# FFN of a hybrid encoder block in two parts of its width, with 36 pairs of its row blocks by seven products of sums

## The chip, the cores and the metric

The kernel runs on one core of one Trainium2 chip. The metric is the device time of one execution in microseconds (us). PE is TensorE, whose weight loads have rows of their own (PEld); DVE is VectorE, ACT is ScalarE, POOL is GpSimd, and SP issues most transfers (its queue is SPq).

## What is computed

One encoder block over x (1 x 256 x 2048, fp32): a pre-RMSNorm, one wide projection, a Hyena branch (long convolution with filters from a small network) and a gated SGU branch, merged by sigmoid gates and a projection, then the feed-forward part that most of the change is about:

```python
h = _rmsnorm(x, norm_ffn_g[l])
gate, up = jnp.split(jnp.einsum('bsd,df->bsf', h, w_ffn_in[l]), 2, axis=-1)
x = x + jnp.einsum('bsf,fd->bsd', jax.nn.silu(gate) * up, w_ffn_out[l])
...
return _rmsnorm(x, norm_final_g)
```

D_MODEL is 2048 and D_FF is 5632, so `w_ffn_in` is 2048 x 11264 and `w_ffn_out` is 5632 x 2048. The 256 tokens are two blocks of 128 (tt = 0, 1).

## The kernel before

**Every product is three products.** An fp32 operand is written as two fp32r parts, hi (a cast, ACT) and lo (the operand less hi, DVE), and a product is hi x hi + hi x lo + lo x hi, accumulated in one PSUM bank of 128 x 512. `Net.tokens` (L127 to L134) issues these three matmuls for each token block: the stationary operand is a 128 x 128 block of the activations, the moving one a 128 x 512 block of the weights.

**Weights are a stream.** `Net.halves` lists every 128 x 1024 piece of weights in the order of use. `Net.feed` (L70 to L87) loads a piece by SP into a buffer `raw` and splits it by `split_to` (L65 to L68: the cast on ACT is L67, the subtraction on DVE L68) into `whi` and `wlo`. `Net.take(i)` (L89) first feeds five pieces beyond i. From the merge on there are six `raw` and six `whi`/`wlo` buffers (four in one pool and two in another, taken in turn), so that the split of piece k waits until PE has read piece k - 6, and the load of piece k until piece k - 6 has been split. Engines work through their instructions in order.

**Stages.** (1) `phase_a` (L452): the SGU half of the projection while x arrives, with its first row block of weights in two pieces of 512 columns, and then all other tiles of the projection, with the filters (`filt`, L509) and convolutions woven in by `hook`, one step at each tile. (2) The branch merge and the output projection (up to L367); each column block of the result is transposed on PE (`turn`, L155 to L162) through two of four `aux` banks, scaled and split into X2. (3) FFN in: 22 chunks, each with 256 columns of gate and 256 of up and 16 row blocks (`line_of`, L136). The chunks use two pairs of banks, `mm` and `mg`, in turn (`banks`, L291), so that a finished pair is read (silu on ACT, L391, the product with up on DVE, L392) while PE fills the other. Two chunks together are transposed two ticks later (a tick is the end of a weight piece in the loop) and split into H. (4) FFN out: four column blocks of 512, each over all 44 row blocks of H. In the last one the last four pieces are kept, so that token block 0 ends early. (5) The last RMSNorm: the sum of squares (L434), a reciprocal square root on DVE, four scalings and stores.

Of the kernel before, what the change touches and what calls it, by code (L numbers as in the profile page):

```python
# [38 lines left out]
class Net:  # L39
    def __init__(self, nc, tc, a):  # L40
        self.nc, self.tc, self.a = nc, tc, a
        self.halves = []
        self.parts = {}
        self.split_at = 0
        self.ws2 = None
        self.todo = []

# [21 lines left out]

    def feed(self, upto):  # L70
        nc = self.nc
        while self.split_at < min(upto, len(self.halves)):
            i = self.split_at
            src, w, kept = self.halves[i]
            pool, n = (self.ws, RAW_BUFS) if self.ws2 is None or i % 3 else (self.ws2, 2)
            raw = pool.tile([P, 1024], F32, name="raw", bufs=n)[:, 0:w]
            nc.sync.dma_start(out=raw, in_=src)
            if kept is None:
                pool, n = (self.ws, HL_BUFS) if self.ws2 is None or i % 3 else (self.ws2, 2)
                hi = pool.tile([P, 1024], F32R, name="whi", bufs=n)[:, 0:w]  # L80
                lo = pool.tile([P, 1024], F32R, name="wlo", bufs=n)[:, 0:w]
                self.split_to(hi, lo, raw)
                self.parts[i] = (hi, lo)
            else:
                hi, lo, view = kept()
                self.split_to(hi, lo, view(raw))
            self.split_at += 1  # L87

# [59 lines left out]
    def tick(self):  # L148

        for t in self.todo:  # L150
            t[0] -= 1
        while self.todo and self.todo[0][0] <= 0:
            self.todo.pop(0)[1]()
# [64 lines left out]

RAW_BUFS = 4
# [5 lines left out]
def build(nc, tc, a):  # L225
# [28 lines left out]
    fi_first = [net.line(a["wfi"][c], 8) for c in range(HF)]  # L254
    fo_first = [net.line(a["wfo"][n], HF) for n in range(4)]

    with ExitStack() as top:
        const = top.enter_context(tc.tile_pool(name="const", bufs=1))
        net.ws = top.enter_context(tc.tile_pool(name="ws", bufs=1))
        ev = top.enter_context(tc.tile_pool(name="ev", bufs=1))  # L260
        dram = top.enter_context(tc.tile_pool(name="dram", bufs=1, space=bass.MemoryType.DRAM))
        gate_d = dram.tile([8, 2, P, 512], F32, name="gate_d")
        y_d = dram.tile([2, P, D], F32, name="y_d")

# [12 lines left out]
        left = ExitStack()  # L277
        ys_pool = left.enter_context(tc.tile_pool(name="ys_pool", bufs=1))
# [57 lines left out]
        for n in range(4):  # L336
# [4 lines left out]
            if n == 0:  # L341

                net.line_of(ps, wo_first[0], 8, M, net.tick)
                left.close()
                x2s = ExitStack()
                x2pool = x2s.enter_context(tc.tile_pool(name="x2pool", bufs=1))
                X2 = x2pool.tile([P, KD, 512], F32R, name="X2")
            else:
                net.line_of(ps, wo_first[n], 8, M, net.tick)
            for tt in range(2):  # L350
# [18 lines left out]
        def rms(which, tts):  # L369

            n = len(tts)
            ms = ev.tile([P, n], F32, name="ms", bufs=2)
            nc.vector.tensor_reduce(out=ms, in_=ss[:, which, tts[0]:tts[0] + n, :], op=ALU.add, axis=AX.X)
            nc.vector.tensor_scalar(out=ms, in0=ms, scalar1=1.0 / D, scalar2=EPS, op0=ALU.mult, op1=ALU.add)
            return net.rsqrt_cols(ev, ms, n)
# [3 lines left out]
        H, two = None, []  # L379
        for c in range(HF):  # L380
            ps = banks()
            net.line_of(ps, fi_first[c], 8, X2, net.tick)
            if c == 0:
                inner.close()
                hpool = sd.enter_context(tc.tile_pool(name="hpool", bufs=1, side="right"))
                H = hpool.tile([P, NF, 512], F32R, name="H")
                nc.vector.tensor_copy(out=r2, in_=rms(0, (0, 1)))
            hs = []
            for tt in range(2):
                h = ev.tile([P, L], F32, name="t", bufs=T_BUFS)  # L390
                nc.scalar.activation(out=h, in_=ps[tt][:, 0:L], func=AF.Silu, scale=r2[:, tt:tt + 1])  # L391
                nc.vector.scalar_tensor_tensor(out=h, in0=ps[tt][:, L:2 * L], scalar=r2[:, tt:tt + 1], in1=h,  # L392
                                               op0=ALU.mult, op1=ALU.mult)
                hs.append(h)

            def to_h(pt, c=c):
                net.split_to(H[:, 2 * c:2 * c + 2, 0:L], H[:, 2 * c:2 * c + 2, L:2 * L], pt)
            two.append((hs, to_h))
            if c % 2:
                net.later(2, lambda two=two: net.turn([t[0] for t in two], [t[1] for t in two]))  # L400
                two = []

        for n in range(4):
            ps = banks()
            cut = HF if n < 3 else HF - TAILQ
            for q in range(cut):
                hi, lo = net.take(fo_first[n] + q)
                for e in range(2):
                    k = 2 * q + e
                    net.tokens(ps, hi, lo, 512 * e, H, k, k == 0, k == NF - 1)  # L410
                net.tick()
            if n == 0:
                x2s.close()
                gfp = sd.enter_context(tc.tile_pool(name="gfp", bufs=1))
                yacc = gfp.tile([P, 2, D], F32, name="yacc")
                for tt in range(2):
                    nc.sync.dma_start(out=yacc[:, tt, :], in_=y_d[tt])
                gB = gfp.tile([P, D], F32, name="gfB")
                nc.sync.dma_start(out=gB, in_=a["gfin"].partition_broadcast(P))
            sl = slice(512 * n, 512 * (n + 1))  # L420
            if n == 3:

                parts = [net.take(fo_first[n] + q) for q in range(cut, HF)]
            for tt in range(2):
                if n == 3:
                    for q in range(cut, HF):
                        hi, lo = parts[q - cut]
                        for e in range(2):
                            k = 2 * q + e
                            net.tokens(ps, hi, lo, 512 * e, H, k, False, k == NF - 1, (tt,))  # L430
                y = yacc[:, tt, sl]
                nc.vector.tensor_tensor(out=y, in0=ps[tt], in1=y, op=ALU.add)
                sq = ev.tile([P, 512], F32, name="sq", bufs=2)
                nc.scalar.activation(out=sq, in_=y, func=AF.Square, accum_out=ss[:, 1, tt, n:n + 1])  # L434
                if n < 3:
                    nc.vector.tensor_tensor(out=y, in0=y, in1=gB[:, sl], op=ALU.mult)
                else:

                    r = rms(1, (tt,))
                    for m in (0, 3, 1, 2):  # L440
                        y = yacc[:, tt, 512 * m:512 * (m + 1)]
                        if m == 3:
                            nc.vector.scalar_tensor_tensor(out=y, in0=y, scalar=r[:, 0:1], in1=gB[:, sl],
# [531 lines left out]
```

## Time and profile before

| | |
|---|---|
| median of 3 runs | 1389.6 us (1389.49 to 1389.66) |
| the profiled execution's own time | 1391.37 us |
| its span, first to last instruction | 1389.6 us |
| PE busy | 1376.4 us (99%), 6570 matmul records |
| weight loads (PEld) busy | 1151.7 us (83%) |
| DVE busy | 867.6 us (62%) |
| ACT busy | 658.1 us (47%) |
| moved by DMA | 276 MB, 199 GB/s on average |

A busy share is a mean over all stages. A matmul's record is longer than the distance to the next one (they overlap in the array), so the cost of a matmul is read from that distance. "Idle before" tells how long an engine had nothing to do ahead of an instruction, and the arrow names what it waited for.

### The profile page before, as it was taken

What the parts mean: (1) busy time and instruction counts of PE and PEld (TensorE: products, weight loads), DVE (VectorE), ACT (ScalarE), POOL (GpSimd) and SP (SyncE); (2) the same over time, 40 slices, a digit from 0 to 9 for tenths busy, and PEclk for the clock granted to TensorE, in tenths of its full rate; (3) what the DMA queues carried; (4) which work ended last, traced back from release to release, by engine and by line L of the source; (5) the groups of instructions that cost most, each with busy time, mean ns of one, the idle gap of its engine ahead of it and who ended that gap; (6) DMA issues with size and microseconds to landing.
All of it is one profiled execution on the core that took longest, in us unless ns stands there. A gap on an engine that the chain in (4) does not pass through costs nothing.

```text
span 1389.6 us, 17294 instructions
## 1 busy us (share of the span) xinstructions
PE 1376.4 (99%) x6570; PEld 1151.7 (83%) x6570; DVE 867.6 (62%) x1191; ACT 658.1 (47%) x819; POOL 0.7 (0%) x6
## 2 busy tenths in 40 slices
PE   9999999999999999999999999999999999999997
PEld 7888888888888888888888888888888888888885
DVE  7887798797888666556555554545455544545453
ACT  7665555555455444445444444444444443434342
POOL 0000000000000000000000000000000000000000
PEclk9999999999999999999999999999999999999999
DMA  8775656556555796677666665656565667666651
GB/s 293 243 240 179 189 173 200 153 184 219 166 164 170 253 317 200 205 231 213 195 184 190 187 194 187 194 184 196 186 192 183 195 219 251 197 188 194 194 182 60
DMA packets 82162, 276.00 MB, mean 199 GB/s; under 512 B 10144, under 2 KB 10912, under 8 KB 81696
## 3 DMA queue, kind: packets, MB, share of 16 engines
q1 hardware_dynamic: 79632, 270.64, 61.3%
q10 hardware_dynamic: 2448, 4.27, 0.8%
q8 instruction: 51, 0.84, 0.2%
q14 instruction: 31, 0.25, 0.0%
HBM read 266.49 MB, written 8.39 MB: 198 GB/s over the span
## 4 chain that ended last, share of the span: by engine, by line
PE 97%; DMA 1%; DVE 1%; ACT 0%; SPq 0%; issue 0%; ACTq 0%
PE mg L132 15%; PE mg L134 15%; PE mg L133 15%; PE mm L133 11%; PE mm L134 11%; PE mm L132 11%; PE mm L98 9%; PE mm L100 4%; PE aux L578 2%; PE aux L162 1%; PE aux L527 1%; PE aux L133 1%; PE aux L134 1%; PE aux L132 0%; DMA raw<-in_wsv 0%; PE aux L613 0%
## 5 line engine op out<-in xcount | busy, mean ns | idle before, releaser
L68 DVE TENSOR_TENSOR wlo<-raw,whi 128x1024 fp32r<-128x1024 f32 (+1 forms) x473 | 577.3, 1222 | 464.9 <-ACT whi L67 459.6
L67 ACT CAST whi<-raw 128x1024 fp32r<-128x1024 f32 (+1 forms) x473 | 496.5, 1051 | 619.9 <-PE mg L134 264.2
L132 PE MATMUL mg<-whi,X 128*128 128x512 f32 x608 | 237.9, 391 | 0.0
L134 PE MATMUL mg<-whi,X 128*128 128x512 f32 x608 | 236.9, 390 | 0.0
L133 PE MATMUL mg<-wlo,X 128*128 128x512 f32 x608 | 236.8, 389 | 0.0
L98 PE MATMUL mm<-X,whi 128*128 128x512 f32 x512 | 161.9, 397 | 0.0
L134 PE MATMUL mm<-whi,X 128*128 128x512 f32 x384 | 150.0, 391 | 0.0
L133 PE MATMUL mm<-wlo,X 128*128 128x512 f32 x384 | 149.9, 390 | 0.0
L132 PE MATMUL mm<-whi,X 128*128 128x512 f32 x384 | 149.7, 392 | 0.0
L134 PEld LDWEIGHTS mg<-whi,X 128*128 128x128 f32 x608 | 114.1, 188 | 24.0
L132 PEld LDWEIGHTS mg<-whi,X 128*128 128x128 f32 x608 | 114.1, 188 | 23.1 <-issue 0.4
L133 PEld LDWEIGHTS mg<-wlo,X 128*128 128x128 f32 x608 | 114.2, 188 | 22.8
L100 PEld LDWEIGHTS mm<-X,wlo 128*128 128x128 f32 x512 | 96.2, 188 | 22.6
L100 PE MATMUL mm<-X,wlo 128*128 128x256 f32 x512 | 100.8, 278 | 0.0
L134 PEld LDWEIGHTS mm<-whi,X 128*128 128x128 f32 x384 | 72.4, 188 | 15.1
L133 PEld LDWEIGHTS mm<-wlo,X 128*128 128x128 f32 x384 | 72.4, 189 | 14.8
L132 PEld LDWEIGHTS mm<-whi,X 128*128 128x128 f32 x384 | 72.1, 188 | 14.7
L98 PEld LDWEIGHTS mm<-X,whi 128*128 128x128 f32 x512 | 79.0, 189 | 1.7 <-issue 0.7
L132 PE MATMUL mm<-whi,H 128*128 128x512 f32 x176 | 68.6, 389 | 0.0
L134 PE MATMUL mm<-whi,H 128*128 128x512 f32 x176 | 68.5, 389 | 0.0
L133 PE MATMUL mm<-wlo,H 128*128 128x512 f32 x176 | 68.5, 389 | 0.0
L132 PE MATMUL mg<-whi,H 128*128 128x512 f32 x176 | 68.5, 389 | 0.0
(228 smaller groups left out, 1598.3 us busy)
## 6 DMA issues: line engine op xcount, KB each, us to landing
raw<-in_wfi SPq DMA_DIRECT2D x176, 512.0 KB, 3.5
raw<-in_wfo SPq DMA_DIRECT2D x88, 512.0 KB, 3.5
raw<-in_wg SPq DMA_DIRECT2D x64, 512.0 KB, 4.0
raw<-in_win SPq DMA_DIRECT2D x64, 512.0 KB, 4.0
raw<-in_wbr SPq DMA_DIRECT2D x32, 512.0 KB, 5.1
raw<-in_wout SPq DMA_DIRECT2D x32, 512.0 KB, 3.9
raw<-in_wsv SPq DMA_DIRECT2D x15, 512.0 KB, 5.5
gate_d<-sq ACTq DMA_DIRECT2D x16, 256.0 KB, 4.5
```

What stands on the lines that cost most here:

```text
L67: self.nc.scalar.copy(out=hi, in_=src)
L68: self.nc.vector.tensor_tensor(out=lo, in0=src, in1=hi.bitcast(F32), op=ALU.subtract)
L98: nc.tensor.matmul(ps[:, 0:512], lhsT=hi[:, col:col + P], rhs=mov, start=start, stop=False)
L100: nc.tensor.matmul(ps[:, 0:256], lhsT=lo[:, col:col + P], rhs=mov[:, 0:256], start=False, stop=stop)
L132: self.nc.tensor.matmul(ps[tt], lhsT=xh, rhs=wh, start=start, stop=False)
L133: self.nc.tensor.matmul(ps[tt], lhsT=xh, rhs=wl, start=False, stop=False)
L134: self.nc.tensor.matmul(ps[tt], lhsT=xl, rhs=wh, start=False, stop=stop)
L162: self.nc.tensor.transpose(out=pt[:, b, tt * P:(tt + 1) * P], in_=src[tt][:, b * P:(b + 1) * P], identity=self.ident)
L527: nc.tensor.matmul(ps.rearrange("p d c -> p (d c)"), lhsT=h3s[:, par_ * P:(par_ + 1) * P], rhs=w, start=(part == 0), stop=(part == 1))
L578: nc.tensor.matmul(ps[:, ri, :], lhsT=fw[:, m + ri, :], rhs=z, start=(n == 0), stop=(n == 2))
```

## The change

**Seven products for a pair of row blocks.** Two row blocks (2 x 128 rows), two token blocks and two column blocks of 512 make a 2 x 2 by 2 x 2 block product: eight block products of three matmuls each. For 36 such pairs the change computes seven, of sums of blocks: four sums of the activations (`forms`), made once for each pair and kept beside the plain blocks (XE for FFN in, HE for FFN out), and three sums of the weights, made on DVE from the pieces as they arrive (`Net.quads`), each piece then split as before. A pair with seven products has pieces of 1024, 1024, 1024 and 512 columns where a plain pair has two of 1024. The names of the products are those of `TAGS`: P2, N3, Q4 and E accumulate over a whole chunk and also take the plain pairs' products of their quadrant (`plain`), in the four banks `mm` and `mg`; P1, Q5, P7 and P6 hold the seven-product pairs alone, in the four `aux` banks. After a chunk's last seven-product pair `sums` combines these four into T and D; at the chunk's end four copies on ACT and two additions on DVE (`finish`) give the result.

**Two parts.** FFN in now runs in chunks of 512 columns of gate and 512 of up (11 of them), eight pairs in each, the third and the sixth of the order by seven products (`PLAN_IN`). After six chunks FFN out runs over the first 24 row blocks of H, in two column blocks of 1024 (12 pairs, four of them by seven: `PLAN_OUT[0]`), and its result goes to memory (p_d). After the other five chunks it runs over the other 20 row blocks (10 pairs, three by seven); `yacc` and the stored parts are loaded at the start of it, added, and the last RMSNorm follows as before. 36 = 11 x 2 + 2 x 4 + 2 x 3.

**Beside this.** In `filt` the bias term is made from one matmul of 128 x 256 with ones in place of two with the identity. In `phase_a` the first three row blocks of weights (`HALVED`) come in halves, not the first alone, and x is loaded in other steps.

```diff
+    def quads(self, src, seven):
...
+        def one():
+            for n in (1, 4, 3, 2):
+                r[n] = self.raw_tile()
+            nc.sync.dma_start(out=r[1], in_=src[0])
+            nc.sync.dma_start(out=r[4][:, 512:1024], in_=src[1][:, 512:1024])
+            nc.sync.dma_start(out=r[3][:, 0:512], in_=src[1][:, 0:512])
+            nc.vector.tensor_tensor(out=r[2].rearrange("p (c n) -> p c n", c=2), in0=r[1].rearrange("p (c n) -> p c n", c=2),
+                                    in1=r[4][:, 512:1024].unsqueeze(1).to_broadcast([P, 2, 512]), op=ALU.add)
+            return self.split(r[1], 1024)
+
+        def two():
+            nc.vector.tensor_tensor(out=r[3][:, 512:1024], in0=r[2][:, 0:512], in1=r[1][:, 512:1024], op=ALU.add)
+            return self.split(r[2], 1024)
+
+        def three():
+            nc.vector.tensor_tensor(out=r[4][:, 0:512], in0=r[3][:, 0:512], in1=r[3][:, 512:1024], op=ALU.add)
+            return self.split(r[3], 1024)
+        for fn in (one, two, three, lambda: self.split(r[4], 512)):
+            self.halves.append((fn, None, None))
...
+class Quad:
+    TAGS = dict(P2="mm", N3="mm", Q4="mg", E="mg", P1="aux", Q5="aux", P7="aux", P6="aux")
...
+    def plain(self, w, k, tts=(1, 0)):
+        for tt in tts:
+            for n, c in ((("E", 512), ("Q4", 0)) if tt else (("N3", 512), ("P2", 0))):
+                self.mul(n, w, c, self.at(k, tt))
+
+    def seven(self, at, j, slot):
+        net = self.net
+        w = net.take(at)
+        self.mul("P1", w, 0, self.at(2 * j, 0))
+        self.mul("N3", w, 512, self.form(slot, 0))
+        w = net.take(at + 1)
+        self.mul("Q5", w, 0, self.form(slot, 1))
+        self.mul("P7", w, 512, self.form(slot, 3))
+        net.tick()
+        w = net.take(at + 2)
+        self.mul("P2", w, 0, self.at(2 * j + 1, 0))
+        self.mul("P6", w, 512, self.form(slot, 2))
+        w = net.take(at + 3)
+        self.mul("Q4", w, 0, self.at(2 * j + 1, 1))
+        net.tick()
+
+    def sums(self):
...
+        nc.scalar.copy(out=t[:, 1, :], in_=b["P1"])
+        nc.vector.tensor_tensor(out=t[:, 0, :], in0=b["P6"], in1=t[:, 1, :], op=ALU.add)
+        nc.vector.tensor_tensor(out=t[:, 2, :], in0=b["P7"], in1=t[:, 0, :], op=ALU.add)
+        nc.vector.tensor_tensor(out=d, in0=b["Q5"].unsqueeze(1).to_broadcast([P, 2, 512]), in1=t[:, 0:3:2, :], op=ALU.subtract)
...
+def forms(net, fx, x, extra, slot):
...
+    nc.vector.tensor_tensor(out=e[:, 1, :], in0=x21, in1=x22, op=ALU.subtract)
+    nc.vector.tensor_tensor(out=e[:, 2, :], in0=e[:, 1, :], in1=x11, op=ALU.subtract)
+    nc.vector.tensor_tensor(out=e[:, 0, :], in0=e[:, 2, :], in1=x12, op=ALU.add)
+    nc.vector.tensor_tensor(out=e[:, 3, :], in0=x11, in1=x21, op=ALU.subtract)
+    net.split_to(extra[:, slot, 0], extra[:, slot, 1], e)
...
+PLAN_IN = plan((0, 1, 2, 3, 5, 4, 6, 7), (2, 4))
+PLAN_OUT = [plan(range(12), (2, 4, 6, 8)), plan(range(10), (2, 4, 6))]
+CHUNKS = (6, 5)
...
+                def to_h(j, H=H, HE=HE, slots=dict(PLAN_OUT[part])):
+                    def sink(pt):
+                        slot = slots[j]
+                        if slot is not None:
+                            x = fx.tile([P, 2, L], F32, name="xf")
+                            nc.scalar.copy(out=x, in_=pt)
+                            pt = x
+                        net.split_to(H[:, 2 * j:2 * j + 2, 0:L], H[:, 2 * j:2 * j + 2, L:2 * L], pt)
+                        if slot is not None:
+                            forms(net, fx, pt, HE, slot)
+                    return sink
+                net.later(4, lambda pq=pq, c=c, f=to_h: net.turn([[pq[:, tt, L * b:L * (b + 1)] for tt in range(2)] for b in range(2)],
+                                                                 [f(2 * c + b) for b in range(2)]))
...
+                if part == 1 and n == 0:
...
+                    for tt in range(2):
+                        nc.sync.dma_start(out=yacc[:, tt, :], in_=y_d[tt])
+                        nc.sync.dma_start(out=other[tt], in_=p_d[tt])
+                    nc.sync.dma_start(out=gB, in_=a["gfin"].partition_broadcast(P))
...
+        nc.tensor.matmul(ps[:, 0:CB], lhsT=ones, rhs=ab[:, 0, :], start=True, stop=True)
...
-            nc.tensor.matmul(ps[0:1, t * P:(t + 1) * P], lhsT=nb[:, t:t + 1], rhs=ident, start=True, stop=True)
...
+HALVED = 3
```

**The order on PE, where a chunk's result has just been transposed.** Before, in FFN in and FFN out (a number behind a name is the buffer's; `t` is the gated product, `ident` the identity), one weight piece after the transposes:

```order
L162 MATMUL aux_9797<-ident_73,t_9748 128x128
L162 MATMUL aux_9797<-ident_73,t_9751 128x128
L132 MATMUL mm_9754<-whi_9696,H_6396 128x512
L133 MATMUL mm_9754<-wlo_9697,H_6396 128x512
L134 MATMUL mm_9754<-whi_9696,H_6396 128x512
```

Now, after the fourth piece of a chunk (`pq` is the gated product), the same place with the seven-product pair that follows:

```order
L203 MATMUL aux_7055<-ident_71,pq_6631 128x128 x4
L203 MATMUL aux_7060<-ident_71,pq_6631 128x128 x4
L283 MATMUL aux_7084<-whi_6955,X2_5694 128x512
L283 MATMUL mm_6996<-whi_6955,XE_5695 128x512
L283 MATMUL aux_7097<-whi_6984,XE_5695 128x512
L283 MATMUL aux_7101<-whi_6984,XE_5695 128x512
L283 MATMUL mm_7000<-whi_7005,X2_5694 128x512
L283 MATMUL aux_7114<-whi_7005,XE_5695 128x512
```

These are the first matmuls of P1, N3, Q5, P7, P2 and P6, each of which has three. What moved: the transposes are now followed, nine and fifteen matmuls later, by products (P7 in aux_7101 and P6 in aux_7114) that take over the two `aux` banks of the transposes, which are taken in turn.

**The order on DVE at the same place.** Before, a split of weights, the two halves of H, and the next split:

```order
L68 TENSOR_TENSOR wlo_9459<-raw_9456,whi_9458 128x1024
L68 TENSOR_TENSOR wlo_9491<-raw_9488,whi_9490 128x1024
L68 TENSOR_TENSOR H_6396<-aux_9474,H_6396 128x2x256
L68 TENSOR_TENSOR H_6396<-aux_9479,H_6396 128x2x256
L68 TENSOR_TENSOR wlo_9509<-raw_9506,whi_9508 128x1024
```

Now, where the transposed block belongs to a pair of FFN out that goes by seven (`xf` is its copy by ACT, `xe` the four forms):

```order
L69 TENSOR_TENSOR wlo_7040<-raw_7037,whi_7039 128x1024
L69 TENSOR_TENSOR wlo_7081<-raw_7078,whi_7080 128x1024
L366 TENSOR_TENSOR xe_7069<-xf_7065 128x128
L369 TENSOR_TENSOR xe_7069<-xf_7065 128x128
L69 TENSOR_TENSOR H_6623<-xf_7065,H_6623 128x2x256
L367 TENSOR_TENSOR xe_7069<-xe_7069,xf_7065 128x128
L69 TENSOR_TENSOR H_6623<-aux_7060,H_6623 128x2x256
L368 TENSOR_TENSOR xe_7069<-xe_7069,xf_7065 128x128
```

What moved: the subtraction that frees the second `aux` bank (the row with aux_7060) now stands behind a weight split, three forms and the other half of H.

**The order on DVE in FFN out,** from one seven-product pair (pieces raw_8899 to raw_8902) over a plain one to the next (raw_9020 to raw_9023); before, nothing but splits stood there, as in the first two rows of the fence on H above:

```order
L69 TENSOR_TENSOR wlo_8954<-raw_8901,whi_8953 128x1024
L69 TENSOR_TENSOR wlo_8974<-raw_8900,whi_8973 128x512
L114 TENSOR_TENSOR raw_9023<-raw_9020,raw_9021 128x1024
L119 TENSOR_TENSOR raw_9022<-raw_9023,raw_9020 128x512
L69 TENSOR_TENSOR wlo_8992<-raw_8989,whi_8991 128x1024
L123 TENSOR_TENSOR raw_9021<-raw_9022 128x512
L69 TENSOR_TENSOR wlo_9010<-raw_9007,whi_9009 128x1024
L69 TENSOR_TENSOR wlo_9029<-raw_9020,whi_9028 128x1024
```

What moved: the first addition of a seven-product pair stands ahead of the two splits of the plain pair before it, and directly behind the last split of the previous seven-product pair, whose buffer (raw_8900) the load of raw_9021 reuses.

## Rows read from the trace of the kernel before

**Rows 1.** The page: span, busy time by engine, and granted clock in 40 slices.
```profile
span 1389.6 us, 17294 instructions
PE 1376.4 (99%) x6570; PEld 1151.7 (83%) x6570; DVE 867.6 (62%) x1191; ACT 658.1 (47%) x819; POOL 0.7 (0%) x6
...
PEclk9999999999999999999999999999999999999999
```

**Rows 2.** The chain by time, FFN in: transposes that end two pairs of chunks (start us, us, what).
```profile
789.35 0.88 PE aux L162 x8
833.76 0.87 PE aux L162 x8
```

**Rows 3.** Who waited for whom, longest first (us in total, times, longest us).
```profile
DVE wlo L68 <- ACT whi L67: 459.6, 371, 2.4
ACT whi L67 <- PE mg L134: 264.2, 166, 2.4
```

**Rows 4.** Stretches: stretch, us, PE, PEld, DVE, ACT, POOL busy, clock, DMA, GB/s.
```profile
800.00:1000.00 200.00, 200.00 (x900) 165.94 (x900) 102.32 (x99) 87.33 (x98) 0.00 (x0) 1.00 0.59 191
```

**Rows 5.** Groups by line and shape (busy us, mean ns, idle before).
```profile
L68 DVE TENSOR_TENSOR wlo<-raw,whi 128x1024 fp32r<-128x1024 f32 x471 | 575.9, 1224 | 464.3 <-ACT whi L67 459.0 <-PE aux L578 4.7
L67 ACT CAST whi<-raw 128x1024 fp32r<-128x1024 f32 x471 | 495.2, 1052 | 619.4 <-PE mg L134 264.2 <-PE mm L134 244.1 <-PE mm L98 45.2
...
L68 DVE TENSOR_TENSOR H<-aux,H 128x512 fp32r<-128x512 f32 x22 | 14.1, 682 | 0.0
...
L67 ACT CAST H<-aux 128x512 fp32r<-128x512 f32 x22 | 11.8, 587 | 0.0
...
L535 DVE TENSOR_TENSOR s2k<-kk 128x512 f32<-128x512 f32 x8 | 5.5, 687 | 0.1
...
L642 DVE TENSOR_TENSOR t<-evb 128x128 f32<-128x128 f32 x8 | 2.3, 285 | 0.0
```

**Rows 6.** Timeline in FFN in, after transposes (start us, us, instruction, idle before).
```profile
833.80 1.05 ACT L67 CAST whi<-raw 128x1024 fp32r<-128x1024 f32 x1 [1.67 <-PE mm L134]
834.75 1.07 ACT L67 CAST H<-aux 128x512 fp32r<-128x512 f32 x2
834.88 1.23 DVE L68 TENSOR_TENSOR wlo<-raw,whi 128x1024 fp32r<-128x1024 f32 x1 [1.49 <-ACT whi L67]
836.02 1.28 DVE L68 TENSOR_TENSOR H<-aux,H 128x512 fp32r<-128x512 f32 x2
```

**Rows 7.** DMA issues (count, KB each, median us from issue to landing).
```profile
raw<-in_wfo SPq DMA_DIRECT2D x88, 512.0 KB, 3.5
...
yacc<-y_d SPq DMA_DIRECT2D x2, 1024.0 KB, 6.2
...
raw<-in_G SPq DMA_DIRECT2D x1, 256.0 KB, 2.6
```

**Rows 8.** The start: timeline of PE and DVE.
```profile
8.14 0.39 PE L134 MATMUL mm<-whi,X 128*128 128x512 f32 x1
10.11 0.73 PE L132 MATMUL aux<-whi,X 128*128 128x512 f32 x2 [1.57 <-ACT whi L67]
...
24.45 1.22 DVE L68 TENSOR_TENSOR wlo<-raw,whi 128x1024 fp32r<-128x1024 f32 x1
...
26.07 0.82 PE L132 MATMUL aux<-whi,X 128*128 128x512 f32 x2
```

**Rows 9.** The start by stretches, columns as in rows 4.
```profile
12.00:14.00 2.00, 2.00 (x6) 1.60 (x5) 1.74 (x3) 2.00 (x4) 0.00 (x0) 0.50 1.03 411
14.00:16.00 2.00, 2.00 (x7) 1.55 (x6) 1.59 (x3) 2.00 (x4) 0.00 (x0) 0.67 1.04 413
```

**Rows 10.** The chain by time: one filter's identity matmuls, and the tail.
```profile
108.78 0.53 PE aux L555 x4
...
1379.50 0.70 DVE yacc L432
1380.22 0.73 ACT sq L434 x2
```

More of the change, by code (lines that the diff above doesn't have):

```diff
@@ L87, in feed @@
-            self.split_at += 1
+            if w is None:
+                self.parts[i] = src()
+            else:
+                raw = self.raw_tile()[:, 0:w]
+                nc.sync.dma_start(out=raw, in_=src)
+                if kept is None:
+                    self.parts[i] = self.split(raw, w)
+                else:
+                    hi, lo, view = kept()
+                    self.split_to(hi, lo, view(raw))
+            self.split_at += 1
+    def quads(self, src, seven):
+        nc, first, r = self.nc, len(self.halves), {}
+        if not seven:
+            return self.line(src, 2)
+        def one():
[15 more added lines that the diff above has]
+            self.halves.append((fn, None, None))
+        return first
@@ L151, in tick @@
             t[0] -= 1
-        while self.todo and self.todo[0][0] <= 0:
-            self.todo.pop(0)[1]()
+        due, self.todo = [t for t in self.todo if t[0] <= 0], [t for t in self.todo if t[0] > 0]
+        for t in due:
+            t[1]()
     def turn(self, srcs, sinks):
@@ L219, with plan @@
+def plan(pairs, seven):
+    return [(j, seven.index(j) if j in seven else None) for j in pairs]
+PLAN_IN = plan((0, 1, 2, 3, 5, 4, 6, 7), (2, 4))
+PLAN_OUT = [plan(range(12), (2, 4, 6, 8)), plan(range(10), (2, 4, 6))]
+CHUNKS = (6, 5)
 RAW_BUFS = 4
@@ L253, in build, with quads @@
     wo_first = [net.line(a["wout"][n], 8) for n in range(4)]
-    fi_first = [net.line(a["wfi"][c], 8) for c in range(HF)]
-    fo_first = [net.line(a["wfo"][n], HF) for n in range(4)]
+    def quads(src, pl):
+        return [net.quads(src[j], slot is not None) for j, slot in pl]
+    fi_first, fo_first = [], []
+    for part in range(2):
+        for c in range(CHUNKS[part]):
+            fi_first.append(quads(a["wfi"][c + 6 * part], PLAN_IN))
+        for n in range(2):
+            fo_first.append(quads(a[f"wfo{part}"][n], PLAN_OUT[part]))
     with ExitStack() as top:
@@ L374, in rms @@
             nc.vector.tensor_scalar(out=ms, in0=ms, scalar1=1.0 / D, scalar2=EPS, op0=ALU.mult, op1=ALU.add)
-            return net.rsqrt_cols(ev, ms, n)
+            return net.rsqrt_cols(fx, ms, n)
         r2 = const.tile([P, 2], F32, name="r2")
[L379 to L415, printed above, removed]
-                for tt in range(2):
[L417 to L440, printed above, removed]
@@ L919, in _lines, with _quads @@
     return w.reshape(k // (2 * P), 2, P, n // 512, 512).transpose(3, 0, 2, 1, 4).reshape(n // 512, k // (2 * P), P, 1024)
+def _quads(w, c1, c2, pl):
+    q = np.stack([w[:, c:c + 512].reshape(-1, 2, P, 512) for c in (c1, c2)], 1)
+    out = np.empty((q.shape[0], 2, P, 1024), np.float32)
+    for j, slot in pl:
+        for r in range(2):
+            out[j, r, :, :512] = q[j, 0, r]
+            out[j, r, :, 512:] = q[j, 1, r if slot is None else 1 - r]
+    return out
 def kernel(**inputs):
```

219 lines of the change are left out of this document (177 added, 42 removed).

## Prediction

> **What bounds the kernel now.** First the busy shares [rows 1]: PE is at work for 1376.4 us of a span of 1389.6, at the full clock in every slice, while DVE has 62% and ACT 47%. That alone doesn't say that PE is the bound, since its records overlap, so the chain of waits comes next. In FFN in, the transposes that end one pair of chunks start 44.41 us after those of the pair before [rows 2]; between them stand 192 matmuls of 512 columns and the transposes' own 0.87 us, so one matmul costs (44.41 - 0.87) / 192 = 0.2268 us, without a gap. The waits say the same from the other side [rows 3]: ACT's weight casts wait for PE to give a buffer back (166 times in one of the two bank sets), and DVE's subtractions wait for those casts. DVE is busy 102.3 us in 200 of FFN in [rows 4]. So PE's stream of matmuls is the time, at 0.2268 us each, and weights are split as far ahead as six buffers allow.
>
> A figure beside this: the Trainium skill (TensorE: Matmul & The Clock Gate, section "Wait — 56ns, not 53.3ns?") gives 215.7 ns between 512-column matmuls at full clock. The trace differs, with 226.8; by the page the saving below would be 23.3 us instead of 24.5.
>
> **What goes.** 36 pairs lose one block product of three matmuls: 108 matmuls x 0.2268 = **-24.5 us**, all on PE. The order on PE has 3060 FFN matmuls where 3168 stood, and 88 FFN transposes as before. Everything else is a question of whether other engines keep up.
>
> **DVE's load.** A plain pair costs two splits, 2 x 1.224 = 2.45 us [rows 5], in 24 x 0.2268 = 5.44 us of PE. A pair by seven costs 3.5 splits (4.28) and the weight sums: one of 1024 columns (taken as a split's 1.224) and two of 512 (0.687 each [rows 5]), 6.88 us in 21 x 0.2268 = 4.76 us of PE. So such a pair is slower on DVE than on PE, and must live on what was split ahead. A chunk of FFN in: six plain pairs 14.7, two by seven 13.8, `sums` 2.6, `finish` 2.45, gating about 1.5, H 1.4, forms 4 x 0.285 + 0.68 = 1.8 [rows 5]: 38.2 us in 186 x 0.2268 + 0.87 = 43.1 us of PE, 89%. A block of FFN out of twelve pairs: 8 x 2.45 + 4 x 6.88 + 5 = 52 us in 62.6, 83%. DVE stays below PE in each stage. It can be behind for a while: the buffers hold six pieces, so a piece can be ready up to 8 us of PE early in the dense part and 13 us elsewhere. ACT's chunk is 18 casts of 1.052, two of about 0.6 and some eleven copies and activations of 0.6 to 0.7: 27 of 43 us.
>
> Two places are tight.
>
> (a) **The `aux` banks after the transposes.** P7 and P6 start nine and fifteen matmuls, 2.04 and 3.40 us, after the transposes' end, in the transposes' banks. Before, a split and then the two halves of H followed there as well [rows 6]: the transposes end at 833.76 + 0.87 = 834.63 [rows 2], ACT casts a weight piece until 834.85, then H; DVE splits the piece until 836.11 and is through with H at about 836.70 and 837.30, 2.07 and 2.67 us after the end. Four of the eleven turns keep this work: P7 is late by 0.03 and a semaphore, say 0.1 us. In the other seven, P7 needs only ACT's copy (about 0.7 us after the end), but the second bank comes free after the split (1.48), two forms (2.05), one half of H (2.73), a form (3.02) and the other half (3.70): P6 waits about 0.3 us. 4 x 0.1 + 7 x 0.3 = **+2.5 us**. No row shows this wait. Its ends are 0 (the forms hidden by idle DVE time) and 11 x 1.4 = 15 us (DVE one split, 1.22 us, behind each time); I take 2.5, since DVE's split there starts when PE gives back a buffer, which catches DVE up.
>
> (b) **The first sum of a seven-product pair in FFN out.** It reads a load into a buffer that the last split of the previous such pair has just freed, and it stands on DVE's queue ahead of the plain pair's splits. A load of 256 KB lands 2.6 us after its issue, one of 512 KB after 3.5 [rows 7], so DVE stands idle about 2.75 us: a period of one pair by seven and one plain pair then costs DVE 6.88 + 2.45 + 2.75 = 12.1 us against 10.2 of PE. It loses 1.9 us a period; there are three periods in a block, 5.7 us, against the 8 us that it is ahead. So this is just covered. In FFN in the pairs by seven are two plain pairs apart, and the buffers are free long before. At the start of part 1's FFN out, SP puts five loads of 1 MB (6.2 us each to landing with others beside them [rows 7]) ahead of the next weights, and DVE adds the first of them between two splits. At the 410 GB/s of the start [rows 9] they take 13 us. I take **+1 us** for (b), between 0 and 12.
>
> **The ends and the rest.** Banks of a chunk: E, Q4, N3 and P2 end 9, 6, 3 and 0 matmuls before the chunk does, and the next chunk needs them in that order, so each of the four copies (0.587 [rows 5]) has 2.04 us, enough for four in a row behind one cast. The cover is ACT's idle time; without it up to 2 us per chunk. The first chunk takes the bank set that the output projection has just filled and waits for one addition: **+0.5**. The tail now adds and squares two pieces after the last matmul where one stood (0.70 and 0.73 [rows 10], overlapping): one more addition, 0.7, and 0.2 for two gated scalings on DVE: **+0.9**. Stores and loads of p_d, 4 MB in 276, lie beside PE; SP's 48 more issues too. Filters: two identity matmuls of 128 columns go (0.53 us for both, 8 times [rows 10]) and one of 256 comes: 0, between -4 and +1.
>
> **The start: 0,** between -3 and +1.5. PE pauses from 8.5 to 10.1 us for the second weight piece [rows 8]; soon after, the clock is at 0.50, the 1.2 GHz level, from 12 to 14 us and partly after [rows 9]. Halved pieces shorten the pause, and with it perhaps this stretch (some 8 matmuls at double cost, 1.6 us). But ACT has no gap from 12 to 16 us [rows 9], and the sixth block's subtraction ends at 25.67, only 0.4 us before PE starts on it [rows 8]. A PE that comes 3 us earlier waits there for the same ACT and DVE work. I take nothing.
>
> **The sum.** -24.5 + 2.5 + 1 + 0.5 + 0.9 = -19.6 us. The profiled execution took 1391.37 us of its own, 1.8 more than its span; the median of the runs shown, 1389.6, is equal to the span. So 1371.8 for a profiled one, and **1370.0 us** for the median, a ratio of 0.986. Its own range, from the terms' near ends: 1365 to 1375.
>
> **The rivals.**
> - *More hidden (0.12).* No bank waits and 3 us from the start: 1389.6 - 24.5 + 0.9 - 3 = 1363. For it: DVE idles much of FFN now [rows 4]. Against: the 0.4 us of slack at the start.
> - *Late loads (0.17).* Place (b) is not covered: four blocks with 2 to 3 us each, or the five large loads hold the weights up: 1370 + 10 = 1380. For it: the margin is 2 us of 8. Against: the first addition waits one load's time only.
> - *DVE behind at each turn, slower (0.08).* The bank wait is on DVE's queue, so whatever DVE is behind there PE waits in full, eleven times. Two splits behind: 11 x (2.45 + 0.2) = 29 us on top of the other terms, 1396.6. It decides from 2.3 us per turn (25 us in all). For it: 89% load. Against: between the last split before the transposes and the one after, DVE has over 1 us free each time.
> - *The clock falls (0.05).* After the 1.57 us pause at the start the granted clock was 0.50 for some 3 us [rows 8, 9], 1.6 us lost. If each turn's wait did that: 11 x 1.6 = 17.6, 1387.6, no change. The Trainium skill (TensorE: Matmul & The Clock Gate, section "A second HAM failure mode: psum-queue depth-cycling") describes a kernel that cycled through its PSUM banks and paid for such short pauses. Against: the waits here would be a fifth of that pause.
> - That the change doesn't do what it says: the order on PE shows the 108 gone, so no chance is left for it.
>
> **How the numbers follow.** My forecast has 0.58. A measurement of this kernel can tell a change of about 0.2%, 2.8 us. Faster by more: 0.58 + 0.12 + 0.17 = 0.87; no change: 0.05; slower: 0.08. The range takes in the first three cases with their bounds, 1363 to 1386, and leaves out the rest, 0.13, and what exceeds the bounds.
>
> **What would show it.** Right: FFN matmuls 0.227 us apart, DVE near 82% of the span, waits of PE for DVE only at P6 and P7, 0.1 to 0.5 us long; ACT's casts still mostly waiting for PE. Wrong: PE or its weight loads waiting for wlo or whi (DVE or loads late), SP's loads landing much later than 3 us, a granted clock below 1.00 after the first 20 us, or an idle PE at the ends of chunks.

## The result, and the profile after

The changed kernel takes **1373.28 us** (median of 4 runs, 1371.01 to 1373.65) against 1389.55 (1389.47 to 1389.66) before, a ratio of 0.9879 with a 95% interval of 0.9867 to 0.9892: 16.3 us less, where 19.6 were forecast. The profiled execution took 1373.49 us of its own, near its median, while that of before (1391.37) lies 1.8 above its own; so spans differ by 17.9, more than the medians do.

The page's span, busy and clock rows (they answer to [rows 1]):

```profile
span 1371.7 us, 17635 instructions
...
PE 1355.3 (99%) x6446; PEld 1132.9 (83%) x6446; DVE 1085.6 (79%) x1465; ACT 752.6 (55%) x956; POOL 0.7 (0%) x6
...
PEclk9999999999999999999999999999999999999999
```

The chain in FFN in, two turns (to [rows 2]: now one chunk each), and one chunk as a stretch (columns as in [rows 4]):

```profile
794.80 0.87 PE aux L203 x8
838.07 0.87 PE aux L203 x8
```
```profile
797.05:840.32 43.27, 43.27 (x195) 35.67 (x195) 35.66 (x41) 25.64 (x32) 0.00 (x0) 1.00 0.62 194
```

A chunk takes 43.27 us, 186 x 0.2268 + 0.87 = 43.05 and 0.22 more. DVE has 35.7 of it, so PE is still the bound. The waits of PE's weight loads over the whole span (total, times, longest), without those of the start and of phase A:

```profile
PEld aux L283 <- DVE H L69: 3.4, 11, 0.3
PEld mg L172 <- ACT whi L68: 3.4, 1, 3.4
...
PEld mg L173 <- DVE wlo L69: 0.8, 1, 0.8
...
PEld mg L283 <- DVE yt L524: 0.3, 1, 0.3
```

The first and last rows are the two waits that the prediction named, the `aux` banks at the eleven turns (the transposes that end a chunk) and the first chunk's bank. In FFN nothing waits for a weight. The wait at a turn is one of P7's bank where no forms stand (four turns, 0.26 or 0.27 us each) and one of P6's where they do (seven turns, 0.34 us each); one of each kind, in the timeline of the weight loads:

```profile
711.34 0.19 PEld L283 LDWEIGHTS aux<-whi,XE 128*128 128x128 f32 x1 [0.26 <-DVE H L69]
...
799.00 0.19 PEld L283 LDWEIGHTS aux<-whi,XE 128*128 128x128 f32 x1 [0.34 <-DVE H L69]
```

The second and third rows of the waits were not foreseen and are not in FFN: they are in the branch merge. There the chain in time reads (rows `issue` of 0.01 to 0.05 us left out), in the changed kernel, then in the kernel before:

```profile
467.55 0.42 SPq L477
468.02 5.23 DMA gt<-gate_d
473.27 6.87 DMA raw<-in_wbr
480.16 1.05 ACT whi L68
481.26 1.22 PE mg L172 x2
```
```profile
470.19 5.62 DMA gt<-gate_d
475.82 5.41 DMA raw<-in_wbr
481.25 1.06 ACT whi L67
482.35 0.73 PE mm L132 x2
```

In both SP issues one weight piece, the late piece below, right behind eight gate loads. Before, PE had other work until 482 and waited 0.32 us; now it stands still. PE in that place (timeline, idle time and releaser in brackets), and the stretch behind it:

```profile
477.93 0.39 PE L174 MATMUL mm<-whi,ysgu 128*128 128x512 f32 x1
481.26 1.22 PE L172 MATMUL mg<-whi,yhy 128*128 128x512 f32 x2 [2.94 <-ACT whi L68]
482.52 0.80 PE L173 MATMUL mg<-wlo,yhy 128*128 128x512 f32 x1
...
485.67 0.63 PE L172 MATMUL mg<-whi,yhy 128*128 128x512 f32 x1
486.10 0.63 PE L173 MATMUL mg<-wlo,yhy 128*128 128x512 f32 x1
...
488.02 0.39 PE L172 MATMUL mg<-whi,yhy 128*128 128x512 f32 x1
488.25 0.39 PE L173 MATMUL mg<-wlo,yhy 128*128 128x512 f32 x1
```
```profile
480.00:485.00 5.00, 3.70 (x8) 2.50 (x9) 3.76 (x4) 4.83 (x5) 0.00 (x0) 0.59 0.65 255
485.00:490.00 5.00, 5.00 (x18) 3.99 (x17) 3.23 (x3) 1.05 (x1) 0.00 (x0) 0.72 0.98 345
```

After 2.94 us of idle time matmuls stand 0.43 us apart for 6.5 us, the 1.2 GHz level (granted clock 0.59 and 0.72 in the two stretches), 14 records where 3.2 us would do: 3.3 lost on top. Some 0.4 of that is a wait for the split of the same piece: the third matmul starts at 482.52, 0.83 us and not 0.43 after the second.

In these two traces phase A had gained before that, as the last start of the casts of yhy shows (form, count, ns, first to last start), before and after:

```profile
L67 ACT CAST yhy<-t x8: 396/406/408, 224.2 to 466.7; 128x256 fp32r<-128x256 f32 x8
```
```profile
L68 ACT CAST yhy<-t x8: 398/406/407, 223.2 to 464.5; 128x256 fp32r<-128x256 f32 x8
```

All in all, by the timeline's starts of the first transposes of the merge and of PE's last matmul:

```profile
500.09 1.03 PE L162 MATMUL aux<-ident,t 128*128 128x128 f32 x8
...
1379.07 0.39 PE L134 MATMUL mg<-whi,H 128*128 128x512 f32 x1
```
```profile
503.67 1.03 PE L203 MATMUL aux<-ident,t 128*128 128x128 f32 x8
...
1360.38 0.39 PE L283 MATMUL mg<-whi,H 128*128 128x512 f32 x1
```

| us | before | after | e1 | e2 | e3 | e6 | e9 | e10 |
|---|---|---|---|---|---|---|---|---|
| to the first transposes | 500.1 | 503.7 | 498.4 | 499.3 | 499.1 | 497.0 | 497.0 | 497.4 |
| from there to the last matmul | 879.0 | 856.7 | 856.8 | 879.4 | 854.7 | 857.0 | 854.6 | 853.4 |
| from there to the span's end | 10.5 | 11.3 | 11.4 | 11.0 | 11.3 | 11.2 | 11.2 | 12.2 |

The first row ends inside the merge; the second is the rest of it, the output projection and FFN, and is called FFN from here on. So FFN gave 22.3 us, the tail took 0.8, and what lies ahead took 3.6: phase A 2.2 faster, the merge 5.8 slower.

### The profile page after: what moved, and what is told of

Its sections match the earlier page's. It is cut to its first block, busy times and chain, and to the rows that moved or that the text cites. A ratio compares the mean times of both kernels' runs of the same rounds, so it can differ in the third digit from the quotient of the medians.

```text
span 1371.7 us, 17635 instructions
## 1 busy us (share of the span) xinstructions
PE 1355.3 (99%) x6446; PEld 1132.9 (83%) x6446; DVE 1085.6 (79%) x1465; ACT 752.6 (55%) x956; POOL 0.7 (0%) x6
## 4 chain that ended last, share of the span: by engine, by line
PE 93%; DVE 3%; DMA 2%; ACT 1%; issue 1%; SPq 0%; DVEq 0%; ACTq 0%
PE mm L283 21%; PE mg L283 20%; PE mm L138 9%; PE aux L283 7%; PE mg L172 6%; PE mg L173 6%; PE mg L174 6%; PE mm L140 4%; PE mm L174 2%; PE mm L173 2%; PE mm L172 2%; PE aux L783 2%; PE aux L203 1%; DVE wlo L69 1%; DMA raw<-in_wsv 1%
## 5 line engine op out<-in xcount | busy, mean ns | idle before, releaser
L68 ACT CAST whi<-raw 128x1024 fp32r<-128x1024 f32 (+1 forms) x547 | 553.0, 1019 | 523.8 <-PE mm L283 201.9
L69 DVE TENSOR_TENSOR wlo<-raw,whi 128x1024 fp32r<-128x1024 f32 (+1 forms) x547 | 640.1, 1179 | 233.9 <-ACT whi L68 222.1
L283 PE MATMUL mm<-whi,X 128*128 128x512 f32 x572 | 201.2, 389 | 0.0
L283 PE MATMUL mg<-whi,X 128*128 128x512 f32 x572 | 197.8, 390 | 0.0
L283 PEld LDWEIGHTS mg<-whi,X 128*128 128x128 f32 x572 | 107.4, 188 | 22.6 <-DVE yt L524 0.3
L283 PEld LDWEIGHTS mm<-whi,X 128*128 128x128 f32 x572 | 107.4, 188 | 22.3
L140 PEld LDWEIGHTS mm<-X,wlo 128*128 128x128 f32 x512 | 96.2, 188 | 22.6
L283 PE MATMUL mm<-wlo,X 128*128 128x512 f32 x286 | 111.3, 389 | 0.0
L172 PE MATMUL mg<-whi,X 128*128 128x512 f32 x256 | 101.1, 395 | 0.0
L174 PE MATMUL mg<-whi,X 128*128 128x512 f32 x256 | 99.8, 391 | 0.0
L283 PE MATMUL mm<-whi,H 128*128 128x512 f32 x268 | 93.9, 389 | 0.0
L283 PEld LDWEIGHTS mm<-wlo,X 128*128 128x128 f32 x286 | 53.7, 188 | 11.2
L283 PEld LDWEIGHTS mg<-wlo,X 128*128 128x128 f32 x286 | 53.7, 188 | 11.2
L283 PEld LDWEIGHTS mm<-whi,H 128*128 128x128 f32 x268 | 50.3, 188 | 10.4
L283 PEld LDWEIGHTS mg<-whi,H 128*128 128x128 f32 x268 | 50.3, 188 | 10.4
L174 PEld LDWEIGHTS mg<-whi,X 128*128 128x128 f32 x256 | 48.1, 188 | 10.2
```

The costliest lines, as they stand in the source:

```text
L68: self.nc.scalar.copy(out=hi, in_=src)
L69: self.nc.vector.tensor_tensor(out=lo, in0=src, in1=hi.bitcast(F32), op=ALU.subtract)
L140: nc.tensor.matmul(ps[:, 0:256], lhsT=lo[:, col:col + P], rhs=mov[:, 0:256], start=False, stop=stop)
L172: self.nc.tensor.matmul(ps[tt], lhsT=xh, rhs=wh, start=start, stop=False)
L174: self.nc.tensor.matmul(ps[tt], lhsT=xl, rhs=wh, start=False, stop=stop)
L283: self.net.nc.tensor.matmul(ps, lhsT=l, rhs=r, start=(n == 0), stop=(n == self.total[name] - 1))
```

## Experiments

Theory: FFN behaves as forecast, and the merge's loss comes from which `raw` buffer a piece gets. `raw_tile` (L71) counts buffers, and every third goes to a second pool whose memory phase A has held; its load stands on SP behind the gate loads, the first of which SP issues 0.5 us after PE's last matmul of phase A starts (467.55 after 467.05; before, 469.72 after 469.17). `HALVED` adds two buffers at the start, so the count is shifted at the merge. Before, the late piece is the last of the SGU half, and PE's order has hyena pieces ahead of it; now it is the first hyena piece, with nothing to put ahead. Rival: phase A simply ends earlier and meets loads at a fixed time. Times are medians; before was 1389.41 to 1389.66 beside them.

**e1, the rotation of before.**
```diff
-        self.raws = self.pairs_ = -1
+        self.raws, self.pairs_ = 0, -1
```


> The changed kernel with the count of raw buffers started one higher, so that the same weight pieces of the merge go to the second pool as in the kernel before. Theory (rotation): the 3.4 us wait of PE at 478 us and the 0.43 us matmuls after it come from which piece stands behind the gate loads on SP; PE's order becomes that of before there, the wait falls to about 0.3 us, no half clock follows, and the time is 1373.3 - 5.8 = 1367.5 us (1366.5 to 1368.5). Rival (phase A ends 2.2 us earlier and runs into loads whose time is fixed): the wait stays between 2 and 3.4 us, 1371 to 1373.5 us.

Measured: 1368.88 us (ratio 0.9852, 0.9838 to 0.9865), 4.4 less than the changed kernel and 0.4 above the top of its range. The wait fell, not to 0.3, and the clock stayed at 1.00 from 480 to 490:

```profile
PEld mm L172 <- ACT whi L68: 1.7, 1, 1.7
```

The rotation is most of it. PE still stands idle for 1.27 us behind that wait. The rival's fixed time does not explain it: SP issues the late piece 3.0 us earlier than before (472.80 against 475.82). But the piece lands only 1.65 us earlier (479.58 against 481.23), since it takes 6.8 us where 5.4 stood; why it takes longer is not shown.

**e4, the third rotation.**
```diff
+        self.raws, self.pairs_ = 1, -1
```


> As e1_rotation, but the count starts two higher than in the changed kernel: the third possible rotation, in which the late piece is the second of the hyena half, so PE has twelve more matmuls, 2.7 us, ahead of it than in the changed kernel, and no reordering. Theory (rotation): the wait is 3.4 - 2.7 = 0.7 us and the clock stays at 1.00: 1367.5 to 1369 us. Rival (any rotation but that of before costs the wait): 1371 to 1373.5 us.

Measured: 1369.13 us (0.9854, 0.9841 to 0.9868). PE waits 0.8 us, at 1.00 (for the split of the late piece, not for its cast). Only the rotation of the changed kernel pays in full.

**e5, the kernel before in that rotation.**
```diff
-            pool, n = (self.ws, RAW_BUFS) if self.ws2 is None or i % 3 else (self.ws2, 2)
+            pool, n = (self.ws, RAW_BUFS) if self.ws2 is None or (i + 2) % 3 else (self.ws2, 2)
```
(for `raw` alone)

> The kernel before with one thing changed: its raw buffers go to the second pool in the rotation of the changed kernel. Nothing of FFN, filters or start differs. Theory (rotation): PE waits some 3 us for the first hyena piece of the merge, and the clock falls behind it, as in the changed kernel: 1389.6 + 5.8 = 1395.4 us (1393 to 1396.5). Rival (the stall belongs to the changed kernel's earlier phase A): 1389.6 us, no change.

Measured: 1392.68 us (1391.88 to 1395.01; 1.0024, 1.0014 to 1.0033), 3.2 slower with nothing else changed: the cause is shown, its size was too high. The profiled execution (1392.08) waited 1.8 and 0.5 us at a clock of 1.00:

```profile
480.78 0.73 PE L132 MATMUL mg<-whi,yhy 128*128 128x512 f32 x2 [1.83 <-ACT whi L67]
```

The mean granted clock was 0.998 in the four executions at 1391.88 to 1392.12 us and 0.995 to 0.997 in the six at 1393.25 us and above, so these had some stretch at a lower clock; that it lies at the merge, no trace shows.

**e6, the gate loads behind the pieces** (on the changed kernel).
```diff
-        gate_load(0)
...
-            if n + 1 < 4:
-                gate_load(n + 1)
-            gt = gts[n]
...
                 net.line_of(ps, br_first[n][1 - h], 4, (yhy, ysgu)[h], net.tick)
+                if h and n == 0:
+                    gate_load(0)
+                if h and n + 1 < 4:
+                    gate_load(n + 1)
+                gt = gts[n]
```


> The changed kernel, its rotation left, with the eight gate loads of the merge issued after the first half's weight pieces and not ahead of them. Theory: the late piece is late only because 2 MB of gates stand ahead of it on SP's queue; with them behind it, it lands some 5 us earlier, the wait and the half clock go: 1366.5 to 1368.5 us. Rival (the piece waits for the memory of phase A, whatever stands ahead of it, or the gates now come late for DVE): 1371 us or more.

Measured: 1366.88 us (0.9838, 0.9822 to 0.9855), 6.4 less. PE does not wait at the merge at all:

```profile
480.00:485.00 5.00, 5.00 (x24) 4.14 (x23) 1.63 (x2) 2.35 (x3) 0.00 (x0) 1.00 1.03 419
```

DMA is full there (share 1.03, 419 GB/s): it is the order of the transfers, not their sum, that left PE idle.

**e7 and e11, the old filters,** on e1 and on e6.
```diff
-        nc.tensor.matmul(ps[:, 0:CB], lhsT=ones, rhs=ab[:, 0, :], start=True, stop=True)
+            nc.tensor.matmul(ps[0:1, t * P:(t + 1) * P], lhsT=nb[:, t:t + 1], rhs=ident, start=True, stop=True)
```


> As e1_rotation, but the bias term of the eight filters is made as before, by two matmuls with the identity. Theory: the 2.0 us by which phase A gained between its first and its last yhy block is these matmuls: 1367.5 + 2.0 = 1369.5 us (1369 to 1370.5). Rival (the filters lie beside other work and the gain is of the start's halved pieces): 1367.5 us.

Measured: 1369.6 us (0.9857, 0.9842 to 0.9872), 0.7 above e1: between the two. (The 2.0 us of the expectation count from the start's last product, the activations that write vg: 54.3 to 466.7 before and 54.1 to 464.5 now. Between the first and the last yhy block it is 1.2.) PE comes to the merge 1.65 us later than in e1 and waits 0.33 us there, not 1.27. So the rest was lost in the wait, which e11 tests:

> e6_gates_later with the bias term of the filters made as before, by two identity matmuls. e7_old_filters showed only 0.7 us, since PE then waited less at the merge. Theory (the 2 us of the filters are real but lost where PE waits for a load at the merge): with that wait gone they show in full, 1366.9 + 2.0 = 1368.9 us (1368.4 to 1369.6). Rival (the filters are hidden and only the start gained): 1366.9 to 1367.7 us.

Measured: 1368.89 us (0.9851, 0.9837 to 0.9866), 2.0 above e6. The filters are worth 2.0 us, and a wait for loads behind them had hidden most of that. The traces agree: from the vg activations to PE's last matmul of phase A the old filters cost 1.9 to 2.0 us, in e7 against e1 and in e11 against e6.

**e2, all pairs plain,** on e1.
```diff
-PLAN_IN = plan((0, 1, 2, 3, 5, 4, 6, 7), (2, 4))
-PLAN_OUT = [plan(range(12), (2, 4, 6, 8)), plan(range(10), (2, 4, 6))]
+PLAN_IN = plan(range(8), ())
+PLAN_OUT = [plan(range(12), ()), plan(range(10), ())]
```


> As e1_rotation, but every pair plain: same two parts, same chunks of 1024 columns, no product of sums (no forms, sums or bank waits). Theory: 108 matmuls come back at 0.2268 us, 24.5 us, and the bank waits of 3.4 us go: 1367.5 + 24.5 - 3.4 = 1388.6 us (1387.5 to 1389.7), DVE near 62% of the span. Rival (the two parts themselves give or cost something: chunks of four banks, stores and loads of p_d): below 1386 or above 1392 us.

Measured: 1391.06 us (1.0011, 1.0002 to 1.002), 22.2 above e1; the stretch of FFN 879.4 against 856.8. (The time is above the theory's range, as e1 was, and below the rival's 1392.) The seven-product pairs are the gain, and two parts alone cost FFN 0.4.

**e3, P7 and P6 one product later,** on e1.
```diff
         self.mul("Q5", w, 0, self.form(slot, 1))
-        self.mul("P7", w, 512, self.form(slot, 3))
         net.tick()
-        w = net.take(at + 2)
-        self.mul("P2", w, 0, self.at(2 * j + 1, 0))
-        self.mul("P6", w, 512, self.form(slot, 2))
+        v = net.take(at + 2)
+        self.mul("P2", v, 0, self.at(2 * j + 1, 0))
+        self.mul("P7", w, 512, self.form(slot, 3))
         w = net.take(at + 3)
         self.mul("Q4", w, 0, self.at(2 * j + 1, 1))
+        self.mul("P6", v, 512, self.form(slot, 2))
```


> As e1_rotation, but in a pair by seven P7 and P6 each start one product later (P1, N3, Q5, P2, P7, Q4, P6), three matmuls, 0.68 us, more than the wait of 0.3 us for their banks. Theory: the eleven waits of PE for the second aux bank go, -3.4 us: 1364.1 us (1363.3 to 1365). Rival (the two weight pieces are held longer, so casts and splits come later and PE waits for wlo in their place): 1367 to 1370 us.

Measured: 1367.1 us (0.9839, 0.9826 to 0.9853). The eleven waits are gone, and turns stand 43.05 us apart, as reckoned without a gap:

```profile
746.83 0.87 PE aux L203 x8
789.88 0.88 PE aux L203 x8
```

The gain in FFN is 2.1 us, not 3.4: a weight load's wait of 0.3 cost the matmuls behind it only 0.2. The time falls into the rival's range, but the rival's wait is not there: in FFN PE's weight loads wait 0.3 us once, for the first chunk's bank. e1, from which the 3.4 were to go, stood at 1368.88 and not at 1367.5.

**e8, the halves of H twice,** on e1.
```diff
+                        nc.vector.tensor_tensor(out=H[:, 2 * j:2 * j + 2, L:2 * L], in0=pt,
+                                                in1=H[:, 2 * j:2 * j + 2, 0:L].bitcast(F32), op=ALU.subtract)
```


> As e1_rotation, but DVE does each lower half of H twice, 0.68 us more for each of two blocks at each of the eleven turns, in places where a weight split and another subtraction stand between. Theory (whatever DVE is behind at a turn PE waits for in full, and a short pause there costs its length alone): the seven turns with forms wait 0.3 + 0.6 + 1.1 + 0.6 + 0.6 = 3.2 us, the other four 1.5: 28.5 us where 3.4 stood, 1367.5 + 25 = 1392.5 us (1385 to 1395). Rival A (DVE's idle time takes it up): 1368 to 1372 us. Rival B (each pause of 3 us is followed by some 3 us at the half clock, as at the merge, 4.7 us for each of seven): 1420 us or more.

Measured: 1368.54 us (0.9848, 0.9834 to 0.9863), no change to e1. DVE did the work (11.7 us more), but the program as built had another order on PE: P6 stands fourteen matmuls further back, behind Q4 and the next plain products. DVE gives the bank back at 753.43 + 0.68, and PE starts P6 at 754.26:

```profile
753.43 0.68 DVE L589 TENSOR_TENSOR H<-aux,H 128x512 fp32r<-128x512 f32 x1
```
```profile
753.90 0.39 PE L283 MATMUL mm<-wlo,X 128*128 128x512 f32 x1
754.26 0.47 PE L283 MATMUL aux<-whi,XE 128*128 128x512 f32 x1
```

So this says nothing of a PE that waits longer there; what it shows is that known DVE work at a turn can be moved around.

**e9, e6 and e3 together.** Both diffs, on the changed kernel.

> e6_gates_later and the order of products of e3_order together, on the rotation of the changed kernel. The stage from the first transposes of the merge to the last matmul was 857.0 us in e6_gates_later and 854.7 in e3_order. If the two gains are of different stages they add: 1366.9 - 2.1 = 1364.8 us (1364.2 to 1365.6). Rival (what one saves the other has saved too, or the pieces held longer cost something without the slack of the merge): 1366 us or more.

Measured: 1365.08 us (0.9824, 0.9809 to 0.9839): the two add, and it beats both kernels, by 24.6 and 8.2 us.

**e10, two more pairs by seven.**
```diff
-PLAN_OUT = [plan(range(12), (2, 4, 6, 8)), plan(range(10), (2, 4, 6))]
+PLAN_OUT = [plan(range(12), (2, 4, 6, 8)), plan(range(10), (2, 4, 6, 7))]
```


> As e9_gates_and_order, with one more pair by seven in each column block of the second FFN out (pairs 2, 4, 6 and 7): six matmuls fewer. Theory (PE's stream is the time as long as DVE's load in a stage is below its own; DVE was busy 53.4 of 60 us there): 6 x 0.2268 = 1.4 us less, 1363.4 us (1362.8 to 1364.2). Rival (pairs by seven next to each other outrun the six buffers, and PE waits for splits): the same as e9_gates_and_order or up to 4 us more.

Measured: 1364.65 us (1364.49 to 1365.27; 0.9822, 0.9807 to 0.9836), not to be told from e9, and above the theory's range. PE gained 1.2 us and the tail gave 1.0 back: DVE, at 58.3 of 60 us in the second FFN out (e9: 55.0), came later to the last additions:

```profile
1350.78 0.68 DVE L645 TENSOR_TENSOR yacc<-mg,yacc 128x512 f32<-128x512 f32 x1
1351.37 1.41 DVE L653 SCALAR_TENSOR_TENSOR yacc<-yacc,rs_y,gfB 128x512 f32<-128x512 f32 x2
1352.69 0.68 DVE L645 TENSOR_TENSOR yacc<-mg,yacc 128x512 f32<-128x512 f32 x1
```

The second addition of token block 1 stands behind two scalings of block 0, and ends 2.5 us after PE's last matmul starts. In e9 both additions stand behind the two scalings and end 1.5 us after it.

**e12, more work for DVE,** on e9.
```diff
-                    self.parts[i] = self.split(raw, w)
+                    hi, lo = self.parts[i] = self.split(raw, w)
+                    if i >= self.ffn and i % 2 == 0:
+                        nc.vector.tensor_tensor(out=lo, in0=raw, in1=hi.bitcast(F32), op=ALU.subtract)
```


> As e9_gates_and_order, with DVE subtracting one of the two pieces of every plain pair of FFN twice: 96 subtractions more, some 1.14 us each, 109 us on DVE. By the stretches of the changed kernel's trace DVE then has 42.4 of 43.05 us in a chunk of FFN in, 60 of 62.6 in a block of the first FFN out and some 55 of 52.4 in one of the second. Theory (PE waits only where a stage gives DVE more than its own time, and buffers carry the rest): 2 x 2.3 = 4.6 us, 1364.8 + 4.6 = 1369.4 us (1365 to 1373). Rival (what DVE is behind at a turn PE waits for in full, eleven times some 2 us): 1385 us or more.

Measured: 1370.3 us (0.9861, 0.9844 to 0.9877), 5.2 above e9. Stretches of FFN in and of the second FFN out:

```profile
746.00:789.00 43.00, 43.00 (x195) 35.55 (x194) 42.68 (x47) 25.46 (x32) 0.00 (x0) 1.00 0.61 200
1260.00:1320.00 60.00, 59.22 (x258) 47.78 (x257) 59.62 (x58) 31.54 (x37) 0.00 (x0) 1.00 0.63 217
```

With DVE at 42.7 of 43 us PE has no gap in that chunk, and from the first turn to the last it lost 0.7 us against e9; where DVE is full, PE begins to wait. From the last turn to the last matmul it is 3.8 us longer than in e9.

## Why the prediction was right, and where it was not

The time lies in the range and on the forecast's side, 3.3 us above 1370.0. That it came so near is partly luck: the merge took 5.8 us that no term held, and FFN and the filters gave 1.8 and 2.0 more than forecast. By its terms:

- **What goes, -24.5: right.** e2 gives the pairs 22.6 us in FFN, 24.5 less the bank waits, within 0.3. The Trainium skill (TensorE: Matmul & The Clock Gate, section "Wait — 56ns, not 53.3ns?") gives 215.7 ns between such matmuls, which would make an estimate of 23.3; the turns of e3 show (43.05 - 0.87) / 186 = 0.2268 us, so the trace differs from it as before.
- **(a), +2.5: right, in size and place.** P6's bank is late in the seven turns with forms, by 0.34 us (forecast 0.3), and P7's in the four others, by 0.26 or 0.27 (forecast 0.1). These eleven waits cost PE 11 x 0.2 = 2.2 us (e3: 2.1).
- **(b) +1 and the first bank +0.5: too high.** No weight is late in FFN; the bank cost 0.3 once. DVE's load was mis-sized: a chunk has 35.7 us and not 38.2, since its instructions overlap (a split of 1.22 us starts 1.13 before the next, 799.07 to 800.20), and the span 79%, not 82.
- **The tail, +0.9: right** (0.8).
- **Filters, 0: the wrong value in the right bounds.** e11 has -2.0. The row of 0.53 us for both matmuls stood in the chain [rows 10]; there was no reason to call it hidden.
- **The start, 0: probably some 1.3 us too low.** The activations behind its last product (vg) start at 54.1 us where the trace shown had 54.3. But that execution took 1.8 us more than the others of its kernel, with a clock of 0.91 in the first 20 us. In e5, whose start is that of before, the clock is 1.00 there and they start at 52.8. All twelve traces with the new start have them at 53.3 to 54.8. So the new start seems the slower one, which would explain why medians gained less than spans. With it the terms add up to the medians' difference: -22.3 (FFN) + 0.8 (tail) - 2.0 (filters) + 1.3 (start) + 5.8 (merge) = -16.4 us, where 16.3 were measured. The old start at the full clock has one trace, so the 1.3 stays open. (In every execution the own time lies 1.7 to 2.2 us above the span; that the median before equals the span shown, as "The sum" reads it, comes of that one execution being longer.)
- **The step that failed** is "The start": it costed the halved pieces by the time of the start alone, and no term held the merge. The two pieces more also shift the count that chooses buffers, and some 430 us later PE stood still for a load. That cost 5.8 us at the merge, 2.6 of longer waiting and the rest behind it at the half clock. The sign that the prediction named, a clock below 1.00 after 20 us, showed it.

The rows on the start, of the kernel before, e5 and the changed kernel:

```profile
L725 ACT ACTIVATE vg<-aux,rcol x2: 681/686/690, 54.3 to 54.9; 128x512 f32<-128x512 f32 x2
```
```profile
L725 ACT ACTIVATE vg<-aux,rcol x2: 679/684/688, 52.8 to 53.4; 128x512 f32<-128x512 f32 x2
```
```profile
L930 ACT ACTIVATE vg<-aux,rcol x2: 679/684/688, 54.1 to 54.7; 128x512 f32<-128x512 f32 x2
```

The rivals: late loads came true in kind (a load that stands behind others on SP) but in the merge, not in FFN. *DVE behind at each turn* fell, by 82% load; e12 puts its point near a full DVE. *The clock falls* at each turn fell too: through eleven waits of 0.3 us it was 1.00. The Trainium skill (TensorE: Matmul & The Clock Gate, section "A second HAM failure mode: psum-queue depth-cycling") tells of a clock that fell again and again behind short idle times between groups of matmuls; that does not describe these waits. The clock fell once, at the merge, where PE was idle for 2.94 us ahead of 14 matmuls, most of them 0.43 us apart. The Trainium skill (TensorE: Matmul & The Clock Gate, section "HAM oscillation — how this bites in real kernels") tells of a TensorE that waits for a transfer and runs what follows at the low clock; the trace agrees in kind.

## To carry to other kernels

A change of how many buffers are taken early moves every later piece to another buffer; where pools differ in when they come free, look on the queue's order for the first place where the new pool is used. A saving ahead of a wait for a load shows only in part until the wait is gone (0.7 of 2.0 us in e7, all of it in e11), so order transfers by who needs them first. For sums of blocks in place of matmuls, count the other engine's load by stage: near 99% it was still hidden here (e12), where it was full it was not.

## What was not expected of the hardware

The length of a pause did not by itself decide whether the clock fell behind it. At the merge the clock stayed at 1.00 after pauses of 1.27 to 1.46 us (e1, e3, e8) and of 1.83 and 0.53 us (e5), and fell to the half level after 2.94. At the start it fell behind 1.57 us in the kernel before [rows 8, 9]. There e2 had pauses of 0.82 and 0.76 us that end at 15.0 and 16.3 us, and e11 of 1.41 and 0.76 that end at 15.1 and 16.4, and it fell in e2 alone (columns as in [rows 4], first e2, then e11):

```profile
16.00:18.00 2.00, 1.72 (x4) 1.37 (x5) 2.00 (x4) 2.00 (x4) 0.00 (x0) 0.61 1.01 396
```
```profile
16.00:18.00 2.00, 1.63 (x7) 1.35 (x8) 1.36 (x4) 1.59 (x3) 0.00 (x0) 1.00 1.01 402
```

At the merge one such fall, with the wait for a split inside it, made a pause of 2.9 us cost 6.2.
